# The last down projection as seven block products, with the weights' block sums made in DRAM

## The chip, the cores and the metric

The kernel runs on one core of one Trainium2 chip. The metric is the device time of the program in microseconds. Three runs of the kernel before gave a median of 1703.05 us (1701.98 to 1703.95).

## The reference, cut to what matters

The program is two layers of a transformer block on 512 tokens of width 1024, in float32. Each layer has a mixer of four branches (causal attention with forget decay, dilated attention, retention and latent attention, MLA), gates, an output projection, and a feed-forward block:

```
h = rms_norm(x, g_pre_ffn[l])
f = (silu(h @ w_ffn_gate[l]) * (h @ w_ffn_up[l])) @ w_ffn_down[l]     # [512,2816] @ [2816,1024]
x = x + rms_norm(f, g_post_ffn[l])
```

The change concerns the last line of the product, `... @ w_ffn_down[l]`, in the second (last) layer. It is the last matrix product of the program; the norm, the residual sum and the store of the output follow it.

## The kernel before, in words

**Products.** A float32 operand is split in two float32r parts: `hi` is a copy by ACT (ScalarE) and `lo = x - hi` is a subtraction by DVE (VectorE) or, for some tiles, by POOL (GpSimd). A product of two such pairs takes three matmuls (hi hi, hi lo, lo hi), which `mm3` and its relatives issue.

**Weights.** All weights lie in one DRAM array `wts` in the order in which they are used. `w_load` loads them by DMAs on SP's queue into three buffers `raw`, `conversion` splits each into `whi` and `wlo`, and `take` hands out the next tile with two more converted ahead. So SP's queue carries the weights, and among them other transfers, above all `move` (L1060), which copies halves of query and key tiles within SBUF.

**Order of the work.** `collect` runs the main chain of products (projections, gates, output projection, feed-forward block) and, at a spacing, steps of a background list `self.bg` (attention and retention), first in, first out. A scheduler (Tile) then orders each engine's instructions: it places an instruction where, by its own estimate of times, the engine is free and the instruction's inputs are there; it holds to the written order in the stretches that `ordered` marks, on the engines named there. Every engine and every queue then runs its instructions in the order in which they stand.

**POOL's part.** In the first 100 us POOL splits the `lo` of query and key tiles (`split_to`, L484, called by `queries` and `keys`), then of value tiles (`v_split`, L930), then multiplies the attention weights by their reciprocal sums (`normalise`, L653). PE transposes the result (L660). SP's moves of the query and key halves (L1062) wait for the splits. In the feed-forward block POOL also issues accumulating DMAs (`units_load`, L335), which add one weight tile to another while loading.

**The feed-forward block.** The gate and up products already run in seven block products in place of eight (`quarter_products`), for 18 of the 22 tiles of the hidden width; the sums of weights for it come partly by these accumulating DMAs into SBUF, partly from DVE. The hidden tiles are held as float32.

**The last product.** `split_rest` (L1671) splits the 22 hidden tiles, and `finish` (L1693) computes the output in token layout: four column blocks of 256, each for four token blocks over 22 tiles of the hidden width, three matmuls each, so 4 x 4 x 22 x 3 = 1056 matmuls of 256 columns. Squares for the norm are summed after each block; the last block's evacuation (`evac`, c == 3) takes the root, scales, adds the residual `xt` and stores.

Of the kernel before, what the change touches and what calls it, by code (L numbers as in the profile page):

```python
# [16 lines left out]
LAYERS = 2  # L17
# [33 lines left out]
NR = 8  # L51
HQ = 3
AHEAD = 2
LAST_K = ((0, 2), (2, 2), (4, 2), (6, 2), (8, 4), (12, 4), (16, 4), (20, 2))

# [10 lines left out]
def plan():  # L66
# [6 lines left out]
    for l in range(LAYERS):  # L73
# [36 lines left out]
        if l < LAYERS - 1:  # L110
            for d, k0, nk in DOWN:
                add("down", nk, 128, lambda a, l=l, d=d, k0=k0, nk=nk:
                    _ktiles(a["w_ffn_down"][l], k0, nk, np.arange(d * 128, d * 128 + 128)))
        else:
            for c in range(4):
                for k0, nk in ((0, 4), (4, 4), (8, 4), (12, 4), (16, 4), (20, 2)) if c < 3 else LAST_K:
                    add("held" if c == 3 and nk == 2 and k0 < 8 else "downt", nk, 256, lambda a, l=l, c=c, k0=k0, nk=nk:
                        _ktiles(a["w_ffn_down"][l], k0, nk, np.arange(c * 256, c * 256 + 256)))
    return out
# [86 lines left out]
class Builder:  # L206
# [28 lines left out]
    def stream_init(self):  # L235
        self.wi = 0
        self.n_dma = self.n_conv = 0
        self.woff = [0]
        for _, nk, nc, _ in self.plan:
            self.woff.append(self.woff[-1] + 128 * nk * nc)  # L240
        self.raw, self.whl = {}, {}
        self.n_held = 0

# [27 lines left out]
    def conversion(self, lo_engine=None):  # L271
# [6 lines left out]
        kh = (nk + 1) // 2  # L278
        if name == "held":
            kh = nk  # L280
            if self.n_held < 2:
                t2 = self.hp.tile([128, 1024], F32R, tag="fraw", name="held")
                tiles = [(t2[:, 0:512], t2[:, 512:1024])]
            else:
                tiles = [(self.ar(), self.ar())]
            self.n_held += 1
        else:
            hi = self.whi.tile([128, 1024], F32R, tag="whi", name="whi")
            lo = self.wlo.tile([128, 1024], F32R, tag="wlo", name="wlo")
            tiles = [(hi, lo), (hi[:, kh * ncol:], lo[:, kh * ncol:])][:nk]  # L290
        ws = [], []
# [28 lines left out]
    def units_load(self, upto):  # L320

        nc = self.nc
        groups = (FT - CM) // 2
        while self.n_unit <= min(upto, 5 * groups - 1):
            g, n = divmod(self.n_unit, 5)
            if self.n_unit % NR < RB:
                t = self.wraw.tile([128, 1024], F32, tag="raw", name="raw")
            else:
                t = self.hp.tile([128, 1024], F32, tag="fraw", name="raw")
            a11, a21, a12, a22 = (self.ap["wts"][self.woff[i]:self.woff[i + 1]].rearrange("(p n) -> p n", p=128)  # L330
                                  for i in range(self.n_dma + 4 * g, self.n_dma + 4 * g + 4))
# [5 lines left out]
            self.n_unit += 1  # L337
        if upto >= 5 * groups:
# [3 lines left out]
            self.w_load(self.n_dma + upto - 5 * groups)  # L342

    def quarters_ahead(self, n):
# [4 lines left out]
        if not self.q_todo:  # L349
# [3 lines left out]
    def quarters_init(self):  # L353

        groups = (FT - CM) // 2
        self.q_todo, self.q_done, self.q_used = deque(), 0, 0
# [5 lines left out]
        for g in range(groups):  # L362
            self.q_todo.extend(self.quarter_steps(5 * g))

    def quarter_steps(self, u):
        nc = self.nc
        st = {}

        def plain(src):
            hi = self.whi.tile([128, 1024], F32R, tag="whi", name="whi")  # L370
            lo = self.wlo.tile([128, 1024], F32R, tag="wlo", name="wlo")
            nc.scalar.copy(hi, src)  # L372
            nc.vector.tensor_sub(lo, src, hi.bitcast(F32))  # L373
            self.quarter.append((hi, lo))

# [810 lines left out]
    def project(self, l, u):  # L1186
# [52 lines left out]
        for i in range(2):  # L1239
# [344 lines left out]
    def ffn(self, l, u, ps, y, xt=None):  # L1584
# [8 lines left out]
        ops = None  # L1593
        self.quarters_init()
        for m in range(CM):
# [96 lines left out]

    def finish(self, hid, xt):  # L1693

        nc = self.nc
        y = {}
        ss, before = self.small(16), self.small(4)
        gout = [self.a(), self.a()]
        for h in range(2):
            nc.sync.dma_start(gout[h], self.ap["gout"][:, 512 * h:512 * h + 512])  # L1700

        for c in range(4):
            def evac(t, ps, c=c):
                half, o = c // 2, 256 * (c % 2)
                if c % 2 == 0:
                    y[t, half] = self.a()
                j = self.a()
                nc.scalar.activation(j[:, 0:256], ps, AF.Square, accum_out=ss[:, 4 * t + c:4 * t + c + 1])
                nc.vector.tensor_mul(y[t, half][:, o:o + 256], ps, gout[half][:, o:o + 256])
                if c == 2:  # L1710
                    s1 = before[:, t:t + 1]
                    nc.vector.tensor_reduce(s1, ss[:, 4 * t:4 * t + 3], axis=mybir.AxisListType.X, op=ALU.add)
                    nc.vector.scalar_tensor_tensor(s1, s1, 1.0 / D, self.eps[:, t:t + 1], op0=ALU.mult, op1=ALU.add)
                if c == 3:
                    s1, r, t1 = (self.small(1) for _ in range(3))
                    nc.vector.scalar_tensor_tensor(s1, ss[:, 4 * t + 3:4 * t + 4], 1.0 / D, before[:, t:t + 1],
                                                   op0=ALU.mult, op1=ALU.add)
                    for _ in self.root(s1, r, t1):
                        pass
                    for h in range(2):  # L1720
                        f = y[t, h]
                        nc.vector.scalar_tensor_tensor(f, f, r, xt[t, h], op0=ALU.mult, op1=ALU.add)
                        nc.sync.dma_start(self.out[128 * t:128 * t + 128, 512 * h:512 * h + 512], f)

            if c < 3:
                tags = ("b",) * 4 if c % 2 == 0 else ("acc", "acc", "acc", "b")
                for r in self.tm("downt", hid, 256, (4, 4, 4, 4, 4, 2), tags):
                    if r == 3:
                        yield 3
                    else:  # L1730
                        evac(*r)
                continue
            ws = {}
            for k0, nk in LAST_K:
                w = self.take("held" if nk == 2 and k0 < 8 else "downt")
                for k in range(nk):
                    ws[k0 + k] = w[0][k], w[1][k]
            for t in range(4):
                o = self.ps("b")[:, 0:256]
                ts = slice(128 * t, 128 * t + 128)  # L1740
                mm = nc.tensor.matmul
                for k in range(FT):
                    x, w = hid[k], ws[k]
                    mm(o, x[0][:, ts], w[0], start=k == 0, stop=False)
                    mm(o, x[0][:, ts], w[1], start=False, stop=False)
                    mm(o, x[1][:, ts], w[0], start=False, stop=k == FT - 1)
                evac(t, o)
                yield 3

    def build(self):  # L1750
        nc, tc = self.nc, self.tc
        with ExitStack() as ctx:
# [26 lines left out]
            for l in range(LAYERS):  # L1779
# [12 lines left out]
                with tc.tile_pool(name="fraw%d" % l, bufs=NR - RB) as self.hp, tc.tile_pool(name="hid%d" % l, bufs=HQ) as self.hq:  # L1792
                    xt = None
                    if last:
                        xt = {}
                        self.bg.append(("xt", self.to_tokens(x, xt)))
                    hid = self.collect(self.ffn(l, u, ps, x, xt))
                    del u, x
                    hid = self.split_rest(hid)
                    x = self.bring_back()  # L1800
                    if last:
                        self.run(self.finish(hid, {(k // 2, k % 2): x[k] for k in range(KT)}))
                    else:
                        u, x = self.down_block(hid, lambda d: self.vec("post_ffn", 8 * l + d), x,
                                         lambda k: self.vec("pre_mix", 8 * (l + 1) + k))
# [62 lines left out]
```

## Time and profile before

| | |
|---|---|
| median of three runs | 1703.05 us |
| profiled execution, time | 1705.07 us |
| profiled execution, span | 1703.3 us |
| granted TensorE clock, mean | 0.998 of full |
| PE busy / weight loads | 1674.1 us (98%) / 1503.2 us (88%) |
| DVE / ACT / POOL busy | 1086.8 (64%) / 823.0 (48%) / 335.6 us (20%) |
| DMA | 217.47 MB, mean 128 GB/s |

The span is the time from the first to the last instruction of the profiled execution; its time, 1705.07 us, has 1.77 us around it, and is 2.02 us above the median of the runs. Busy shares are means over the span: PE is busy almost everywhere. The other engines, the DMA queues and the waits matter where PE waits for them.

### The profile page before, as it was taken

Reading aid. Unit: us, or ns where it says so; the run is one execution under the profiler, and the core shown is the slowest. Engines: PE = TensorE matmul, PEld = TensorE weight load, DVE = VectorE, ACT = ScalarE, POOL = GpSimd, SP = SyncE. Lnnn points to the kernel's source line nnn. Section 1 sums busy time; section 2 is a strip of 40 time slices with the busy share of each in tenths; the row PEclk is TensorE's granted clock in tenths of the full one; section 3 lists DMA queues with packets and bytes.
Section 4 is the critical chain, followed back from the end, with each engine's and each line's share of the span. In section 5 each row is a group of like instructions: output and inputs, shape, how many; then the busy total and the mean of one; then the engine's idle time right before and its main releaser. Section 6 shows DMA issues by size and latency. Waiting matters only on the chain.

```text
span 1703.3 us, 27371 instructions
## 1 busy us (share of the span) xinstructions
PE 1674.1 (98%) x10340; PEld 1503.2 (88%) x10340; DVE 1086.8 (64%) x2078; ACT 823.0 (48%) x1657; POOL 335.6 (20%) x344
## 2 busy tenths in 40 slices
PE   9999999999999999999998999999999999999998
PEld 7788888888898999988887988788888989999998
DVE  6657777555468777752485578664554787777423
ACT  6566653323455555553355656432334555555422
POOL 0144333222130010000212443422222300000000
PEclk9999999999999999999999999999999999999999
DMA  5633325323434666243245442343234267773421
GB/s 185 191 106 118 100 81 158 96 93 100 157 114 129 185 180 185 87 160 101 65 153 159 116 115 81 100 155 99 93 99 155 63 185 187 182 178 84 165 94 57
DMA packets 75780, 217.47 MB, mean 128 GB/s; under 512 B 9728, under 2 KB 9984, under 8 KB 75648
## 3 DMA queue, kind: packets, MB, share of 16 engines
q1 hardware_dynamic: 70464, 196.85, 36.3%
q0 software_dynamic: 5184, 18.88, 6.5%
q8 instruction: 81, 1.33, 0.3%
q14 instruction: 51, 0.42, 0.1%
HBM read 189.47 MB, written 8.39 MB: 116 GB/s over the span
## 4 chain that ended last, share of the span: by engine, by line
PE 61%; DVE 4%; ACT 1%; issue 1%; DMA 1%; POOL 0%; DVEq 0%; ACTq 0%
PE acc L491 8%; PE acc L492 8%; PE acc L493 8%; PE acc L465 4%; PE acc L467 4%; PE acc L466 4%; PE b L467 3%; PE b L466 3%; PE b L465 3%; PE b L980 1%; PE b L982 1%; PE b L981 1%; PE b L714 1%; DVE wlo L298 1%; PE b L634 1%
## 5 line engine op out<-in xcount | busy, mean ns | idle before, releaser
L491 PE MATMUL acc<-a,whi 128*128 128x512 f32 (+1 forms) x1238 | 478.0, 386 | 0.0
L493 PE MATMUL acc<-a,wlo 128*128 128x512 f32 (+1 forms) x1238 | 469.4, 379 | 0.0
L492 PE MATMUL acc<-a,whi 128*128 128x512 f32 (+1 forms) x1211 | 459.1, 379 | 0.0
L297 ACT CAST whi<-raw 128x512 fp32r<-128x512 f32 (+3 forms) x442 | 237.5, 577 | 392.4 <-issue 162.1
L298 DVE TENSOR_TENSOR wlo<-raw,whi 128x512 fp32r<-128x512 f32 (+3 forms) x442 | 301.2, 713 | 183.2 <-ACT whi L297 182.1
L493 PEld LDWEIGHTS acc<-a,wlo 128*128 128x128 f32 x1238 | 233.3, 188 | 44.1 <-issue 0.5
L491 PEld LDWEIGHTS acc<-a,whi 128*128 128x128 f32 x1238 | 234.0, 189 | 38.7 <-issue 1.0
L492 PEld LDWEIGHTS acc<-a,whi 128*128 128x128 f32 x1211 | 228.6, 189 | 38.8 <-DVE a L487 0.6
L465 PE MATMUL acc<-a,whi 128*128 128x256 f32 x560 | 158.5, 283 | 1.9 <-DVE a L1598 1.5
L466 PE MATMUL acc<-a,whi 128*128 128x256 f32 x560 | 158.4, 283 | 0.0
L467 PE MATMUL acc<-a,wlo 128*128 128x256 f32 x560 | 158.2, 283 | 0.0
L373 DVE TENSOR_TENSOR wlo<-raw,whi 128x1024 fp32r<-128x1024 f32 x90 | 110.2, 1225 | 57.1 <-ACT whi L372 53.5
L372 ACT CAST whi<-raw 128x1024 fp32r<-128x1024 f32 x90 | 94.4, 1049 | 95.1 <-PE acc L466 47.0
L1261 DVE TENSOR_TENSOR a<-acc,a 128x512 f32<-128x512 f32 x64 | 44.2, 691 | 137.2 <-PE acc L493 137.2
L465 PE MATMUL b<-a,whi 128*128 128x256 f32 x448 | 126.8, 283 | 0.0
L466 PE MATMUL b<-a,whi 128*128 128x256 f32 x448 | 126.8, 283 | 0.0
L467 PE MATMUL b<-a,wlo 128*128 128x256 f32 x448 | 126.8, 283 | 0.0
L1280 POOL TENSOR_TENSOR a<-a 128x512 f32<-128x512 f32 x48 | 70.3, 1467 | 237.8 <-DVE a L1279 229.1
L465 PEld LDWEIGHTS acc<-a,whi 128*128 128x128 f32 x560 | 107.4, 192 | 2.3 <-ACT whi L372 1.7
L466 PEld LDWEIGHTS acc<-a,whi 128*128 128x128 f32 x560 | 107.5, 192 | 0.1
L467 PEld LDWEIGHTS acc<-a,wlo 128*128 128x128 f32 x560 | 107.4, 192 | 0.0
L335 POOL DMA_DIRECT2D raw<-wts x36 | 31.2, 868 | 354.8 <-DMA raw<-wts 195.6
(293 smaller groups left out, 3398.0 us busy)
## 6 DMA issues: line engine op xcount, KB each, us to landing
raw<-wts SPq DMA_DIRECT2D x260, 512.0 KB, 3.6
raw<-wts POOLq DMA_DIRECT2D x36, 512.0 KB, 6.2
a<-a SPq DMA_DIRECT2D x120, 128.0 KB, 2.3
raw<-wts SPq DMA_DIRECT2D x40, 256.0 KB, 2.6
a<-xT SPq DMA_DIRECT2D x16, 256.0 KB, 6.4
away<-a SPq DMA_DIRECT2D x16, 256.0 KB, 6.8
a<-away SPq DMA_DIRECT2D x16, 256.0 KB, 4.9
raw<-wts SPq DMA_DIRECT2D x7, 452.0 KB, 3.8
```

The source lines that it names most:

```text
L297: todo.append(lambda hi=hi, src=src, n=n: nc.scalar.copy(hi[:, :n], src))
L298: todo.append(lambda hi=hi, lo=lo, src=src, n=n: (lo_engine or nc.vector).tensor_sub(lo[:, :n], src, hi[:, :n].bitcast(F32)))
L372: nc.scalar.copy(hi, src)
L373: nc.vector.tensor_sub(lo, src, hi.bitcast(F32))
L465: mm(o, hi[:, c], x[k][0], start=first, stop=False, skip_group_check=i in (2, 3, 4, 6))
L466: mm(o, hi[:, c], x[k][1], start=False, stop=False, skip_group_check=i in (2, 3, 4, 6))
L467: mm(o, lo[:, c], x[k][0], start=False, stop=k == 3, skip_group_check=i in (2, 3, 4, 6))
L491: mm(out, w[0], x[0], start=start, stop=False)
L492: mm(out, w[0], x[1], start=False, stop=False)
L493: mm(out, w[1], x[0], start=False, stop=stop)
L1261: nc.vector.tensor_mul(z, ps, self.rB)
L1280: nc.gpsimd.tensor_add(merged[dd], merged[dd], t)
```

## The change

The last product is done by blocks. The 512 tokens are cut into two halves, the 2816 rows of hidden width into two times 11 tiles (`FH`), and the 1024 columns into two times 512. Seven products of one half block each (11 tiles, 2 token blocks of 128, 512 columns, three matmuls: 66 matmuls; 462 in all, of 512 columns) take the place of eight. Four of the seven use sums of weight blocks, called p, q, r and v: p = a21+a22, r = a11+a21, q = p+a11, v = q+a12. `make_sums` makes them in a new DRAM array `sums`: for each sum six DMAs on POOL's queue copy the first term, and six accumulating DMAs add the second (48 DMAs; in each six, five of 512 KB and one of 256 KB, so 5.5 times 512 KB), every one cut into pieces of 256 float32 (`max_dma_last_dim=1024`, 512 rows of 1 KB). They are put on the background list behind the last layer's retention and drained before its feed-forward block. `w_load` no longer serves the last product; `units_load` loads its blocks, the sums among them, as plain tiles from DRAM. The sums of hidden tiles (t1 to t4) are made by DVE in `finish`, whose operands are split product by product, so `split_rest` is not called for the last layer. The residual `xt` comes back from DRAM in the fourth product.

```diff
+OPS = 3
+LATE = 8
+FH = FT // 2
+LAST_K = tuple((k, min(2, FH - k)) for k in range(0, FH, 2))
...
-            for c in range(4):
-                for k0, nk in ((0, 4), (4, 4), (8, 4), (12, 4), (16, 4), (20, 2)) if c < 3 else LAST_K:
...
+            for c, k1 in ((0, 0), (0, FH), (512, 0), (512, FH)):
+                for k0, nk in LAST_K:
+                    add("block", nk, 512, lambda a, l=l, c=c, k=k0 + k1, nk=nk:
+                        _ktiles(a["w_ffn_down"][l], k, nk, np.arange(c, c + 512)))
...
+    def make_sums(self):
+
+        a11, a12, a21, a22 = (self.block_quarter(n) for n in range(4))
+        p, q, r, v = (self.block_sum(n) for n in "pqrv")
+        for dst, first, more in ((p, a21, a22), (r, a11, a21), (q, p, a11), (v, q, a12)):
+            for d, f in zip(dst, first):
+                self.nc.gpsimd.dma_start(d, f, max_dma_last_dim=1024)
+                yield
+            for d, m in zip(dst, more):
+                self.nc.gpsimd.dma_start(d, m, accum_op=ALU.add, max_dma_last_dim=1024)
+                yield
+
+    def block_sources(self):
+        a11, a12, _, a22 = (self.block_quarter(n) for n in range(4))
+        return [*a11, *a12, *self.block_sum("q"), *self.block_sum("r"), *a22, *self.block_sum("p"), *self.block_sum("v")]
...
         self.bg.append(("b%d" % RET, self.retention(self.heads(q, k), v, g, self.br[RET], l)))
+        if l == LAYERS - 1:
+            self.bg.append(("sums", self.make_sums()))
...
+        products = (plain(0, h0), plain(FH, h0), of_t2, of_t3, of_t4, of_t1, plain(FH, h1))
...
+        for n in range(7):
+            first, grouped = n in (0, 1, 5), n in (2, 3, 4, 6)
...
+            for k, nk in steps:
+                operands(OPS)
+                self.quarters_ahead(AHEAD)
+                w = self.quarter.popleft()
...
+                held.append((k, nk, ready.popleft(), w))
+                if k >= LATE:
+                    continue
+                self.block(banks[n], held.pop(), (0, 1), first, grouped)
+            for t in range(2):
+                for x in held:
+                    self.block(banks[n], x, (t,), first, grouped)
+                after(n)(t)
...
+            self.sums = dram.tile([4, 128 * 512 * FH], F32, name="sums")
...
                     if last:
+                        self.drain("sums")
                         xt = {}
```

**POOL, the start of the program.** This is what stood first in POOL's queue before; `a` are the work tiles, `sm1` the reciprocal sums, L484 the splits of queries and keys, L930 those of values, L653 the scaling of attention weights.

```order
L484 TENSOR_TENSOR a_443<-a_440,a_442 128x512 [waits Activation_49]
L484 TENSOR_TENSOR a_517<-a_514,a_516 128x512 [waits Activation_49]
L484 TENSOR_TENSOR a_610<-a_607,a_609 128x512 [waits Activation_49]
L484 TENSOR_TENSOR a_695<-a_692,a_694 128x512 [waits Activation_49,Pool_49]
L930 TENSOR_TENSOR a_811<-a_809,a_811 128x4x64 [waits PE_49,Activation_49]
L930 TENSOR_TENSOR a_816<-a_814,a_816 128x4x64 [waits PE_49,Activation_49]
L930 TENSOR_TENSOR a_889<-a_887,a_889 128x4x64 [waits DMAHW5_49,Activation_49]
L930 TENSOR_TENSOR a_894<-a_892,a_894 128x4x64 [waits Activation_49]
L653 TENSOR_SCALAR a_919<-a_919,sm1_939 128x128 [waits DVE_49,PE_49]
L653 TENSOR_SCALAR a_934<-a_934,sm1_957 128x256 [waits DVE_49]
```

The first split of a query tile was POOL's first work of any length.

Now 34 DMAs of the sums stand ahead of that split (L522 is the old L484). This fence begins with the 31st of the 48; L360 copies, L363 accumulates, and the semaphores DMASW are those of POOL's own DMAs.

```order
L363 DMA sums_86<-wts 512x256 [waits DMASW6_49,DMASW0_49]
L363 DMA sums_86<-wts 512x256 [waits DMASW7_49,DMASW1_49]
L363 DMA sums_86<-wts 512x256 [waits DMASW2_49]
L363 DMA sums_86<-wts 512x256 [waits DMASW3_49]
L522 ISA
L522 TENSOR_TENSOR a_444<-a_441,a_443 128x512 [waits Activation_49]
L363 DMA sums_86<-wts 512x256 [waits DMASW4_49]
L522 TENSOR_TENSOR a_518<-a_515,a_517 128x512 [waits Activation_49]
L363 DMA sums_86<-wts 256x256 [waits DMASW5_49]
```

The scheduler has put the DMAs, which need nothing but weights in DRAM, at the head of POOL's queue in the first layer, though the program writes them in the second. The last of them stand here, with what follows (L968 is the old L930, L691 the old L653):

```order
L522 TENSOR_TENSOR a_611<-a_608,a_610 128x512 [waits Activation_49]
L363 DMA sums_86<-wts 512x256 [waits DMASW5_49]
L363 DMA sums_86<-wts 512x256 [waits DMASW6_49]
L363 DMA sums_86<-wts 512x256 [waits DMASW7_49]
L363 DMA sums_86<-wts 512x256 [waits DMASW0_49]
L363 DMA sums_86<-wts 256x256 [waits DMASW1_49]
L522 TENSOR_TENSOR a_696<-a_693,a_695 128x512 [waits DMAHW0_49,Activation_49]
L968 TENSOR_TENSOR a_812<-a_810,a_812 128x4x64 [waits PE_49,Activation_49]
L968 TENSOR_TENSOR a_817<-a_815,a_817 128x4x64 [waits PE_49,Activation_49]
L968 TENSOR_TENSOR a_890<-a_888,a_890 128x4x64 [waits DMAHW5_49,Activation_49]
L968 TENSOR_TENSOR a_895<-a_893,a_895 128x4x64 [waits PE_49,Activation_49]
L691 TENSOR_SCALAR a_920<-a_920,sm1_940 128x128 [waits DVE_49]
```

All 48 stand ahead of the fourth split and of the first scaling of attention weights; each waits for the DMA eight places ahead of it (or a later one) and, where it accumulates or reads a sum, for the one that wrote it.

**SP, the same place of the program.** Before, the moves of query halves (L1062) stood among the weight loads (L257) thus:

```order
L836 DMA a_467<-ukv 128x512 [waits DMAHW3_49]
L257 DMA raw_533<-wts 128x1024 [waits DMAHW4_49,DVE_49]
L257 DMA raw_621<-wts 128x1024 [waits DMAHW5_49,DVE_49]
L257 DMA raw_706<-wts 128x1024 [waits DVE_49]
L1062 DMA a_520<-a_516 64x512 [waits DMAHW7_49,Activation_49]
L1062 DMA a_520<-a_517 64x512 [waits DMAHW0_49,Pool_49]
L257 DMA raw_714<-wts 128x1024 [waits DMAHW4_49,DMAHW1_49,DVE_49]
L1062 DMA a_516<-a_517 64x512 [waits DMAHW7_49,DMAHW2_49]
L257 DMA raw_897<-wts 128x1024 [waits DMAHW5_49,DMAHW3_49,DVE_49]
```

Now (L1100 is the old L1062, L259 the old L257):

```order
L259 DMA raw_622<-wts 128x1024 [waits DMAHW4_49,DVE_49]
L259 DMA raw_707<-wts 128x1024 [waits DMAHW5_49,DVE_49]
L259 DMA raw_715<-wts 128x1024 [waits DMAHW6_49,DVE_49]
L1100 DMA a_447<-a_444 64x512 [waits Pool_49]
L1100 DMA a_443<-a_444 64x512 [waits DMAHW7_49]
L1100 DMA a_521<-a_517 64x512 [waits DMAHW0_49,Activation_49]
L1100 DMA a_521<-a_518 64x512 [waits DMAHW1_49,Pool_49]
L259 DMA raw_898<-wts 128x1024 [waits DMAHW3_49,DMAHW2_49,DVE_49]
L1100 DMA a_517<-a_518 64x512 [waits DMAHW0_49]
```

The three weight loads stand a little earlier, ahead of the first move that waits for POOL; the loads behind it wait with it.

## Rows read from the trace of the kernel before

**Rows 1.** Who waited for whom: total us, times, longest; PE, whole span.

```profile
PE b L660 <- POOL a L653: 4.7, 6, 1.8
```

**Rows 2.** Timeline of PE near 88 us: start, duration, [idle before it <- releaser].

```profile
87.18 0.44 PE L634 MATMUL b<-a 128*128 128x128 f32 x3
88.75 0.33 PE L660 MATMUL b<-ct,a 128*128 128x128 f32 x1 [1.13 <-POOL a L653]
```

**Rows 3.** Timeline of POOL, first 90 us.

```profile
42.94 2.09 POOL L484 TENSOR_TENSOR a<-a 128x512 fp32r<-128x512 f32 x1 [42.49 <-ACT a L483]
...
74.35 1.29 POOL L484 TENSOR_TENSOR a<-a 128x512 fp32r<-128x512 f32 x1 [5.88 <-ACT a L483]
81.41 1.82 POOL L930 TENSOR_TENSOR a<-a 128x256 fp32r<-128x256 f32 x2 [5.76 <-ACT a L929]
85.36 1.60 POOL L930 TENSOR_TENSOR a<-a 128x256 fp32r<-128x256 f32 x2 [2.14 <-ACT a L929]
88.33 0.37 POOL L653 TENSOR_SCALAR a<-a,sm 128x128 f32<-128x128 f32 x1 [1.37 <-DVE sm L652]
```

**Rows 4.** Timeline of SP's queue, first 100 us.

```profile
59.95 0.33 SPq L257 DMA_DIRECT2D raw<-wts  x1
...
79.39 2.89 SPq L257 DMA_DIRECT2D raw<-wts  x2
```

**Rows 5.** Busy us of each engine, clock, DMA share and GB/s by stretch.

```profile
core 0: us, PE busy (x) PEld busy (x) DVE busy (x) ACT busy (x) POOL busy (x), PEclk, DMA share, GB/s
...
0.00:88.80 88.80, 80.72 (x413) 68.32 (x414) 56.86 (x129) 52.44 (x107) 9.84 (x13) 1.00 0.57 180
```

**Rows 6.** DMA queues of the page: packets, MB, share of 16 engines' span.

```profile
q1 hardware_dynamic: 70464, 196.85, 36.3%
q0 software_dynamic: 5184, 18.88, 6.5%
```

**Rows 7.** Line L335, POOL's accumulating DMAs: ns min/median/max, and us to landing.

```profile
L335 POOL DMA_DIRECT2D raw<-wts x36: 853/862/1021, 283.0 to 1531.9; - x36
...
DMA to landing us min/median/max: 5.2/6.2/9.6
```

**Rows 8.** DMA in 40 slices of 856 to 866 us: busy tenths, GB/s (stores to DRAM).

```profile
DMA  9899878999999999999999999899432110200000
GB/s 410 328 328 344 311 279 344 320 385 410 377 393 385 410 410 402 434 410 393 402 385 377 393 410 369 311 401 410 148 139 98 74 74 0 66 0 0 0 0 0
...
kept<-a SPq DMA_DIRECT2D x8, 256.0 KB, 4.0
```

**Rows 9.** Timeline of PE: a stretch of 512 columns, first and last of 14.

```profile
61.42 0.39 PE L491 MATMUL b<-a 128*128 128x512 f32 x1
...
64.42 0.39 PE L492 MATMUL b<-a 128*128 128x512 f32 x1
```

**Rows 10.** Timeline of PE: first and last matmul of the last product.

```profile
1569.29 0.28 PE L980 MATMUL b<-whi,a 128*128 128x256 f32 x1
...
1696.17 0.28 PE L1746 MATMUL b<-whi,h 128*128 128x256 f32 x1
```

**Rows 11.** Groups of DVE, 1440 us to the end: busy us, mean ns.

```profile
L373 DVE TENSOR_TENSOR wlo<-raw,whi 128x1024 fp32r<-128x1024 f32 x30 | 36.8, 1225 | 19.8 <-ACT whi L372 18.9 <-ACT a L1623 0.4
...
L484 DVE TENSOR_TENSOR a<-a 128x512 fp32r<-128x512 f32 x16 | 10.1, 687 | 0.1
...
L1722 DVE SCALAR_TENSOR_TENSOR a<-a,sm 128x512 f32<-128x512 f32 x8 | 5.7, 749 | 0.1
L1709 DVE TENSOR_TENSOR a<-b,a 128x256 f32<-128x256 f32 x13 | 5.4, 422 | 19.8 <-ACT a L1708 19.6
```

**Rows 12.** Timeline, the last work of DVE.

```profile
1698.72 1.41 DVE L1722 SCALAR_TENSOR_TENSOR a<-a,sm 128x512 f32<-128x512 f32 x2
```

**Rows 13.** Timeline of PE at the program's start.

```profile
5.87 0.74 PE L1002 MATMUL acc<-whi,a 128*128 128x452 f32 x1 [0.50 <-ACT a L1307]
...
10.97 0.58 PE L1003 MATMUL acc<-wlo,a 128*128 128x452 f32 x1
...
11.35 0.58 PE L1004 MATMUL acc<-whi,a 128*128 128x452 f32 x1
...
12.20 0.37 PE L1004 MATMUL acc<-whi,a 128*128 128x452 f32 x1
...
12.40 0.37 PE L1002 MATMUL acc<-whi,a 128*128 128x452 f32 x1
```

More of the change, by code (lines that the diff above doesn't have):

```diff
@@ L278, in conversion @@
         kh = (nk + 1) // 2
[L279 to L290, printed above, removed]
+        hi = self.whi.tile([128, 1024], F32R, tag="whi", name="whi")
+        lo = self.wlo.tile([128, 1024], F32R, tag="wlo", name="wlo")
+        tiles = [(hi, lo), (hi[:, kh * ncol:], lo[:, kh * ncol:])][:nk]
         ws = [], []
@@ L337, in units_load @@
             self.n_unit += 1
-        if upto >= 5 * groups:
+        if upto >= 5 * groups and not self.blocks:
             if self.n_unit == 5 * groups:
@@ L1593, in ffn @@
         ops = None
-        self.quarters_init()
+        self.quarters_init(self.block_sources() if xt is not None else [])
         for m in range(CM):
@@ L1691, in to_tokens, with finish @@
                 yield
-    def finish(self, hid, xt):
+    def finish(self, h):
         nc = self.nc
-        y = {}
-        ss, before = self.small(16), self.small(4)
[L1698 to L1748, printed above, removed]
@@ new lines, in finish, with operands @@
+        products = (plain(0, h0), plain(FH, h0), of_t2, of_t3, of_t4, of_t1, plain(FH, h1))
+        beside = {0: make_t1, 1: make_t2}
+        todo = deque((f, k, nk) for f in products for k, nk in LAST_K)
+        ready = deque()
+        def operands(n):
+            while todo and len(ready) < n:
+                f, k, nk = todo.popleft()
+                ready.append(f(k, nk))
+        chain, other, late = ([self.ps(t), self.ps(t)] for t in ("b", "b", "acc"))
+        banks = (chain, other, chain, chain, chain, late, late)
@@ new lines, in finish, with done @@
+        e = {n: [self.a(), self.a()] for n in (0,)}
+        y, xt = {}, {}
+        ss, before = self.small(16), self.small(4)
+        def done(t, half, src, sign, at):
+            j = self.a()
+            c = 4 * t + half
+            nc.scalar.activation(j, src, AF.Square, accum_out=ss[:, c:c + 1])
+            y[t, half] = self.a()
+            stt(y[t, half], src, sign, gout[half], op0=ALU.mult, op1=ALU.mult)
+            if not at:
+                nc.vector.scalar_tensor_tensor(before[:, t:t + 1], ss[:, c:c + 1], 1.0 / D, self.eps[:, t:t + 1],
+                                               op0=ALU.mult, op1=ALU.add)
+                return
+            s1, r, t1 = (self.small(1) for _ in range(3))
+            nc.vector.scalar_tensor_tensor(s1, ss[:, c:c + 1], 1.0 / D, before[:, t:t + 1], op0=ALU.mult, op1=ALU.add)
+            for _ in self.root(s1, r, t1):
+                pass
+            for i in range(2):
+                f = y.pop((t, i))
+                stt(f, f, r, xt.pop((t, i)), op0=ALU.mult, op1=ALU.add)
+                nc.sync.dma_start(self.out[128 * t:128 * t + 128, 512 * i:512 * i + 512], f)
@@ new lines, in block @@
+    def block(self, banks, step, ts, first, grouped):
+        mm = self.nc.tensor.matmul
+        k0, nk, x, w = step
+        for t in ts:
+            for i in range(nk):
+                c = slice(256 * i + 128 * t, 256 * i + 128 * t + 128)
+                ws = slice(512 * i, 512 * i + 512)
+                last = k0 + i == FH - 1
+                mm(banks[t], x[0][:, c], w[0][:, ws], start=first and k0 + i == 0, stop=False, skip_group_check=grouped)
+                mm(banks[t], x[0][:, c], w[1][:, ws], start=False, stop=False, skip_group_check=grouped)
+                mm(banks[t], x[1][:, c], w[0][:, ws], start=False, stop=last, skip_group_check=grouped)
```

130 lines of the change are left out of this document (113 added, 17 removed).

## The prediction

> **What bounds the kernel now.** I read the page first: PE is busy nearly everywhere, so a saving must come off PE's work, and whatever makes PE wait is added to the time in full. Next I read who waits for whom on PE. Its waits are short, and the one on another engine that the change touches is PE's wait for POOL: the transposes of the attention weights (L660) wait for POOL's scaling (L653), 4.7 us in six waits [rows 1]. So I looked at where that chain begins. PE's first such transpose is at 88.75 us, right behind POOL's first scaling [rows 2]; POOL did little before, and mostly waited for ACT, 42.49 us ahead of its first split [rows 3]. To a scheduler that is a free engine. Then I set the new order of POOL's queue beside these times: 34 of the 48 DMAs of the sums now stand ahead of the split that ran at 42.94 us, and all 48 ahead of the one that ran at 74.35 us. The question of the whole change is when the chip can be done with them. The last stretch I read last: PE goes through the old product without a gap [rows 10].
>
> **The end: what the seven products save.** The old product has 1056 matmuls of 256 columns. The first starts at 1569.29 and the last at 1696.17, 1055 steps of 0.1203 us, so 127.0 us in all [rows 10]. Matmuls of 512 columns follow each other by (64.42 - 61.42) / 13 = 0.2308 us [rows 9]; 462 of them take 106.6 us. PE saves 20.4 us.
>
> DVE gets more to do beside it. Weights: 35 splits of 1024 columns at 1.225 us and 7 of 512 at 0.69, 47.7 us. Operands: three products split plainly, 33 halves at 0.42, and four from sums, 4 x (5 x 0.687 + 0.42), 29.3 us. Sums of hidden tiles: 44 halves at 0.42, 18.5 us. Evacuations: 4 sums at 0.69 and 8 products with the gain at 0.75, 8.8 us [rows 11]. That is 104 us of DVE beside 106.6 us of PE, and the norm and final scaling of the first two token blocks (some 5 us) come on top. DVE is then as full as PE, with a few tiles of lead (three operand sets, two weight tiles), and ACT must come first for each split. I count 6 us of PE's waits for it (0 if the lead covers all, 15 if DVE runs a seventh slower than its sum). The 22 splits ahead of the old product, 22 x 0.687 = 15.1 us, fall away, but PE had not waited for them, so they are worth nothing.
>
> The tail grows. Before, the last matmul ended at 1696.17 + 0.28 and DVE's last instruction at 1698.72 + 1.41, 3.7 us later [rows 10, 12]. Now two token blocks are finished close together, 2 x (0.69 + 0.75 + about 1.1 of small steps + 1.41) = 7.9 us of DVE, of which the first may start nine matmuls (2.1 us) before the end: about 6 us, 2.3 more than before. So the end gives 20.4 - 6 - 2.3 = 12.1 us, between 3 and 18.
>
> **The start: what the sums cost.** POOL runs its queue in order. The fourth split stands behind the last accumulate, and this waits for the sixth copy of v, the 42nd DMA. Up to that one there are four rounds of copies and three of accumulates, each round 5.5 times 512 KB: 22 copies and 16.5 accumulates of 512 KB. No row shows a copy from DRAM to DRAM, nor 1 KB pieces. Bounds for 512 KB with all 16 engines:
>
> Copies. Stores to DRAM in 2 KB pieces move up to 410 GB/s [rows 8], which makes 1.28 us the low end. The high end is the mean packet of the hardware queue, 0.363 x 1703.3 x 16 / 70464 = 0.140 us [rows 6], taken for every 1 KB piece: 512 pieces and 16 completions are 33 packets on each engine, 4.63 us.
>
> Accumulates. The 36 of the old kernel took 0.065 x 1703.3 / 36 = 3.08 us of all engines each, in 144 packets of 0.342 us [rows 6, 7]. Low end 3.08 us (bytes decide), high end 33 x 0.342 = 11.3 us (packets decide).
>
> The 2 KB row shows no loss against the bigger pieces, so I stay nearer the bytes than the packets, but not at them, as each piece is half as long again and both ends are DRAM: 0.067 us a piece for a copy, 2.2 us, and 0.150 for an accumulate, 5.0 us. The sum is 22 x 2.2 + 16.5 x 5.0 = 130.9 us of the DMA engines (78.9 at the low ends, 287.9 at the high ends).
>
> The other traffic goes on beside it until PE stops: the share was 0.57 over the first 88.8 us [rows 5], 50.6 us. The 42nd DMA has then landed at 130.9 + 50.6 = 181.5 us. Behind it on POOL come one issue (0.86 [rows 7]), the fourth split (1.29), the four value splits (3.42) and the first scaling (0.37) [rows 3]: 187.4 us. PE wanted that scaling at 88.75, so it stands still for 98.7 us. What else waits there costs nothing more: SP's weight load that went at 59.95 is now behind a move that waits for POOL's second split, and the next (79.39) behind the fourth [rows 4], but the tiles already loaded reach past PE's stop. A slower first 20 us, with the sums in the loads' way, is hidden too, since POOL is later still. Nor is the wait won back later, because PE has no slack to give.
>
> After such a pause PE may begin at its lower clock. At the start of the program steps of 0.38 us went over to 0.20, as from 1.2 to 2.4 GHz, after about 5.9 us of work [rows 13]; that lost 5.9 x (1 - 0.205 / 0.375) = 2.6 us, and I add it once.
>
> The Trainium skill, page "DMA: Bandwidth & Descriptors", section "Latency and other measured facts", gives 207 to 214 GB/s for well-pitched copies between HBM tensors. By it 512 KB would take 2.45 us; with accumulates dearer by the ratio of the two queues' bytes, 1.87, the estimate for the sums would be 129 us, so nearly the same time; no run so far shows such a copy.
>
> **Sum.** 1705.07 + 98.7 + 2.6 - 12.1 = 1794.3 us for a profiled execution like this one. That execution lay 2.0 us above the median of the runs, so I predict 1792 us.
>
> **Rivals.** *A, the forecast:* the wait at middle prices, 1765 to 1860 us. For it: the order of POOL's queue and the row of PE waiting for POOL.
>
> *B, bytes decide.* At the low ends the 42nd DMA lands at 129.5 us, PE waits 46.7 us, and the time is 1703.05 + 46.7 - 18 = 1732 us. For it speaks the 2 KB row; against it that every piece is 1 KB, and that POOL must write four times as many descriptors: if an issue grows from 0.862 us with the packets (528 against 144, 3.16 us), 44 full issues alone take 139 us and the time is 1750 us.
>
> *C, packets decide.* At the high ends PE waits 255.6 us and the time is 1703.05 + 255.6 + 2.6 - 3 = 1958 us. For it: an accumulate that reads and writes DRAM has a round trip in each piece; against: the 2 KB row.
>
> *D, the other side, faster.* The change does what its background place intends: the sums are over before POOL is needed. That takes all 42 DMAs within 88.75 - 5.9 = 82.8 us, of which the rest uses 50.6, so 32 us for what costs 78.9 at the lowest rows. The end's gain is eaten once the sums take over 44 us. If it came so, the time would be 1703.05 - 12.1 = 1691 us. Only if the busy share of the engines overstates what they were doing could it be.
>
> **How the numbers follow.** A 0.55, B 0.22, C 0.16, D 0.05, and 0.02 for a wait that just cancels the gain. The bounds of the unknown prices run from 1732 to 1958. The range 1735 to 1900 leaves out D, the low tip of B and the upper half of C, together under 0.2. One measurement of this kernel can tell 0.2% (3.4 us) from no change: faster 0.05, same 0.02, slower 0.93.
>
> **What would show it.** Right: PE's first transpose of attention weights has an idle time of 50 us or more in front, released by POOL; POOL's first split comes after 34 DMAs, well past 42.94; the stretch behind is shifted as a whole; the last product takes about 107 to 115 us with steps of 0.23 us; DVE is above 90% busy there. Wrong: POOL's first scaling runs near 88 us (D), or the time between issue and landing of the sums' DMAs is far off 2.2 and 5.0 us per 512 KB in the mean, once the queue is full (B or C), or PE stops for the end's operands rather than for POOL at the start.

## The result, and the profile after

The changed kernel takes 1728.05 us (median of 4 runs) against 1703.14 us beside it: a ratio of 1.0147, 95% interval 1.0134 to 1.016. It is slower, as forecast, but by 25 us and not by 89; the time lies 7 us below the range. The profiled execution took 1727.95 us, with a span of 1726.2.

**The start.** The timeline of POOL answers to [rows 3], in its columns: the first split, the fourth, the first scaling, and ahead of them the last two accumulates (`x2`), of which the second, about 1 us later, waits for the 42nd DMA.

```profile
88.80 1.67 POOL L522 TENSOR_TENSOR a<-a 128x512 fp32r<-128x512 f32 x1
...
118.38 1.93 POOL L363 DMA_DIRECT2D sums<-wts  x2 [0.35 <-DMA sums<-sums]
119.97 1.63 POOL L522 TENSOR_TENSOR a<-a 128x512 fp32r<-128x512 f32 x1
121.19 3.10 POOL L968 TENSOR_TENSOR a<-a 128x256 fp32r<-128x256 f32 x4
123.94 1.15 POOL L691 TENSOR_SCALAR a<-a,sm 128x128 f32<-128x128 f32 x2
```

The first scaling is 35.6 us later than before (88.33). PE's first transpose of attention weights [rows 2] follows it at 124.69:

```profile
124.69 0.47 PE L698 MATMUL b<-ct,a 128*128 128x128 f32 x1 [4.65 <-POOL a L691]
```

PE did not stop for 36 us in one piece, though; the idle time released by POOL is 4.65. It had been slow from the first microseconds. The stretches (the columns of [rows 5]) show it: 33 matmuls in the first 20 us where there were 57, and 308 up to 88.8 us where there were 413, at a granted clock of 0.90.

```profile
0.00:20.00 20.00, 12.41 (x33) 8.09 (x34) 6.06 (x10) 6.05 (x9) 11.34 (x18) 0.96 0.93 305
0.00:88.80 88.80, 69.95 (x308) 57.08 (x309) 44.84 (x106) 40.53 (x80) 27.33 (x39) 0.90 1.08 295
88.80:124.00 35.20, 22.09 (x116) 18.02 (x115) 12.60 (x26) 13.74 (x30) 19.51 (x24) 0.76 1.13 266
```

How much of the delay was there before POOL decided anything is seen at four casts of ACT whose inputs come from PE, not from POOL. Of ACT's line (ns min/median/max, first and last start), before:

```profile
L483 ACT CAST a<-b x4: 581/581/582, 61.6 to 71.1; 64x512 fp32r<-64x512 f32 x4
```

and after:

```profile
L521 ACT CAST a<-b x4: 581/581/582, 80.3 to 90.4; 64x512 fp32r<-64x512 f32 x4
```

They are 19 us late, and POOL's first split began only at 88.80. So some 19 us were lost ahead of POOL, and from there it is POOL that comes last: between 60 and 126 us ACT waits for its split, and PE for the rows that follow from it (total us, times, longest).

```profile
PE b L672 <- DVE a L968: 9.2, 2, 5.8
...
ACT a L967 <- POOL a L522: 6.9, 1, 6.9
```

The DMAs of the first 118.4 us say why, in the queues' columns of [rows 6] and with the median us to landing of three kinds of issue:

```profile
q0 software_dynamic: 12382, 20.64, 76.0%
q1 hardware_dynamic: 5473, 13.62, 32.6%
...
sums<-wts POOLq DMA_DIRECT2D x30, 512.0 KB, 17.1
raw<-wts SPq DMA_DIRECT2D x11, 512.0 KB, 9.9
...
a<-xT SPq DMA_DIRECT2D x8, 256.0 KB, 13.7
```

In the same stretch of the kernel before, x (`a<-xT`) landed after 5.6 us and weights after 4.6:

```profile
raw<-wts SPq DMA_DIRECT2D x16, 512.0 KB, 4.6
...
a<-xT SPq DMA_DIRECT2D x8, 256.0 KB, 5.6
```

Of the whole page, the software queue's row answers to [rows 6]:

```profile
q0 software_dynamic: 20032, 41.95, 12.9%
```

**The end.** First and last matmul of the new product [rows 10], and DVE's last work [rows 12]:

```profile
1604.83 0.40 PE L1890 MATMUL b<-whi,a 128*128 128x512 f32 x1
...
1717.01 0.39 PE L1892 MATMUL acc<-whi,a 128*128 128x512 f32 x1
```

```profile
1721.61 1.41 DVE L1828 SCALAR_TENSOR_TENSOR a<-a,sm 128x512 f32<-128x512 f32 x2
```

The product begins 35.54 us later than before, so of what was lost in the first 124 us nothing was won back, and nothing added to it, in the 1480 us between. From there to the end of the span it takes 1726.2 - 1604.8 = 121.4 us, against 1703.3 - 1569.3 = 134.0: a gain of 12.6.

### The profile page after: what moved, and what is told of

It is laid out like the page before. It is cut to its first block, busy times and chain, and to the rows that moved or that the text cites. A ratio compares the mean times of both kernels' runs of the same rounds, so it can differ in the third digit from the quotient of the medians.

```text
span 1726.2 us, 26398 instructions
## 1 busy us (share of the span) xinstructions
PE 1665.4 (96%) x9746; PEld 1469.8 (85%) x9746; DVE 1130.4 (65%) x2145; ACT 849.7 (49%) x1676; POOL 373.4 (22%) x392
## 4 chain that ended last, share of the span: by engine, by line
PE 59%; DVE 4%; ACT 1%; issue 1%; POOL 1%; DMA 1%; SPq 0%; DVEq 0%; ACTq 0%
PE acc L529 8%; PE acc L530 8%; PE acc L531 8%; PE acc L503 4%; PE acc L505 4%; PE acc L504 4%; PE b L505 3%; PE b L504 3%; PE b L503 3%; PE b L1890 2%; PE b L1892 1%; PE b L1891 1%; PE b L752 1%; DVE wlo L291 1%; PE b L672 1%
## 5 line engine op out<-in xcount | busy, mean ns | idle before, releaser
L290 ACT CAST whi<-raw 128x512 fp32r<-128x512 f32 (+3 forms) x398 | 213.6, 577 | 353.0 <-PE acc L530 154.8
L291 DVE TENSOR_TENSOR wlo<-raw,whi 128x512 fp32r<-128x512 f32 (+3 forms) x398 | 273.9, 719 | 151.2 <-ACT whi L290 150.7
L531 PEld LDWEIGHTS acc<-a,wlo 128*128 128x128 f32 x1238 | 233.9, 189 | 43.9 <-issue 0.5
L529 PEld LDWEIGHTS acc<-a,whi 128*128 128x128 f32 x1238 | 234.4, 189 | 38.6 <-issue 1.0
L405 DVE TENSOR_TENSOR wlo<-raw,whi 128x1024 fp32r<-128x1024 f32 x132 | 157.6, 1195 | 67.8 <-ACT whi L404 63.7
L404 ACT CAST whi<-raw 128x1024 fp32r<-128x1024 f32 x132 | 135.4, 1027 | 127.1 <-PE acc L504 51.2
L521 ACT CAST a<-a 128x512 fp32r<-128x512 f32 (+1 forms) x143 | 77.6, 567 | 75.2 <-DVE a L860 20.4
```

What stands on the lines that cost most here:

```text
L290: todo.append(lambda hi=hi, src=src, n=n: nc.scalar.copy(hi[:, :n], src))
L291: todo.append(lambda hi=hi, lo=lo, src=src, n=n: (lo_engine or nc.vector).tensor_sub(lo[:, :n], src, hi[:, :n].bitcast(F32)))
L404: self.nc.scalar.copy(hi, src)
L405: self.nc.vector.tensor_sub(lo, src, hi.bitcast(F32))
L529: mm(out, w[0], x[0], start=start, stop=False)
L531: mm(out, w[1], x[0], start=False, stop=stop)
```

## Experiments

The theory: the loss is all at the start and the gain all at the end, and POOL's order (its splits and scalings behind the sums' DMAs) makes the loss. The rival: the sums' bytes hold back the loads, whatever POOL's order.

**End only, and start only.** The first takes `make_sums` out and gives the last product plain blocks in place of q, r, p and v:

```diff
-            self.bg.append(("sums", self.make_sums()))
-        return [*a11, *a12, *self.block_sum("q"), *self.block_sum("r"), *a22, *self.block_sum("p"), *self.block_sum("v")]
+        return [*a11, *a12, *a21, *a11, *a22, *a21, *a12]
```

> The changed kernel without the 48 DMAs that make the sums: the last product takes plain blocks (a11, a12, a21, a22) where it took q, r, p and v, so its numbers are not the reference's, but each instruction of the end stands as in the changed kernel. Theory (the loss is all at the start, the end gains what its two traces say, 134.0 - 121.4 = 12.6 us): 1703.1 - 12.6 = 1690.5 us, between 1688 and 1693; the last product begins at about 1569 us and POOL's first split is back at about 43 us. Rival (the end gains nothing, or less, when the work ahead of it is not late): 1700 to 1704 us.

The second adds `make_sums` and its place in `project` to the kernel before, and changes nothing else.

> The kernel before with the 48 DMAs of the sums added at the same place of the program; nothing reads the sums, and the last product is the eight-block one. Theory (POOL runs them ahead of its first split, and everything behind it is late by 35.5 us): 1703.1 + 35.5 = 1738.6 us, between 1734 and 1743; first split at about 89 us, first scaling of POOL at about 124 us (88.33 before). Rival (the DMAs cost nothing by themselves, the loss is in the new last product and its loads): 1703 to 1708 us.

End only: 1688.64 us against 1701.65, ratio 0.9922 (0.9907 to 0.9936). Start only: 1738.04 us, ratio 1.0216 (1.0199 to 1.0233). Their product is 1.0136, inside the interval of the change (1.0134 to 1.016). So there are two parts, -13.0 and +36.4 us, and no third that these runs can tell (the interval is some 4 us wide).

**Held back.** Each sums' DMA is queued behind one of POOL's 48 additions in the gate stages:

```diff
-                        nc.gpsimd.tensor_add(merged[dd], merged[dd], t)
+                        add = nc.gpsimd.tensor_add(merged[dd], merged[dd], t)
+                        with self.tc.issue_after(add.ins):
+                            next(self.todo, None)      # todo = make_sums()
```

> The changed kernel with the 48 DMAs held back: one is queued on POOL behind each of its 48 additions in the two layers' gate stages (about 13.6 us for two of them), in place of all 48 ahead of POOL's first split. All else is the changed kernel's. Theory (it is their place in POOL's order that costs): POOL's first split back at about 43 us, PE no later, 1703.1 - 12.6 = 1690.5 us, up to 1695 if the weights of the gates come a little later beside them; faster than both kernels. Rival (the bytes cost the time wherever they are moved, through the DMA engines that the weights need): 24 x 2.0 + 24 x 3.1 = some 110 us of packets in stages whose share is 0.37 to 0.56 would again show as weights that come late, 1710 to 1728 us. In this run the queue's share while only copies or only accumulates run gives the price of each alone: 2.0 us and 3.1 us for 512 KB if the split made from the changed kernel's totals is right, 2.2 and 5.0 if the forecast's prices were right.

1691.88 us, ratio 0.9937 (0.9922 to 0.9952): faster than both. POOL's first scaling is back at 88.06 us. Here each kind of DMA runs by itself, with the DMA engines about half busy, so each has a price. Software queue, 379.5 to 419.5 us (five copies of 512 KB and one of 256 KB, so five and a half):

```profile
q0 software_dynamic: 800, 2.88, 20.8%
```

and 420 to 520 us (five accumulates and a half):

```profile
q0 software_dynamic: 2912, 2.88, 19.8%
```

A copy of 512 KB takes 0.208 x 40 / 5.5 = 1.51 us of all engines, an accumulate 0.198 x 100 / 5.5 = 3.60: neither the 2.0 and 3.1 expected here nor the forecast's 2.2 and 5.0. The accumulates went in 1 KB packets (5 x 528 + 272 = 2912), the copies did not: 800 packets are 5 x 144 + 80, so 144 a copy, as with 4 KB pieces, though the code asks for 1 KB.

**Early, but spread.** The same with one DMA behind each of POOL's first 48 splits and scalings in the first layer, so that nothing stands ahead of the first split.

> The changed kernel with the 48 DMAs between POOL's instructions of the first layer's attention: one behind each of its first 48 splits and scalings (from about 43 us on), none ahead of the first split. Theory (the wait for POOL behind its DMAs costs, the traffic beside the first loads costs little): POOL never holds more than one DMA ahead of a split, at most some us per DMA where it has eight in flight and has to wait for one; 1691 to 1700 us, the first splits and scalings at about their times of before (43, 74, 88 us). Rival (the traffic itself delays the first layer's loads, whatever POOL's order): 1705 to 1728 us with POOL's splits waiting for ACT and PE, and x and weight loads that land 10 us or more after their issue.

1726.14 us, ratio 1.0139 (1.0124 to 1.0154): my theory's number was wrong, the rival's right. POOL's first scaling ran at 89.01 us, but between 100 and 200 us, where most of the DMAs now were, PE did 419 matmuls in place of 613 (this run, then the kernel before):

```profile
100.00:200.00 100.00, 79.63 (x419) 68.34 (x419) 46.84 (x129) 42.91 (x107) 58.16 (x71) 0.88 1.10 269
```

```profile
100.00:200.00 100.00, 99.07 (x613) 88.36 (x612) 66.65 (x172) 59.73 (x150) 42.69 (x51) 1.00 0.41 116
```

The software queue took 85.3% of that stretch, 128 KB moves (a<-a) landed after 6.2 us in place of 2.3. So POOL's order was not the only cause, and the next runs took order, issue and bytes apart.

**An eighth of the bytes, at the start and early.** 16 of each DMA's 128 rows; first on "start only", then on "early" (there with the plain blocks of "end only"):

```diff
-                self.nc.gpsimd.dma_start(d, f, max_dma_last_dim=1024)
+                self.nc.gpsimd.dma_start(d[:16], f[:16], max_dma_last_dim=1024)
```

> The kernel before with the 48 DMAs at the start, as in the run of the start alone (1738.0 us), but each moves an eighth of its bytes (16 of 128 rows, 64 KB in place of 512 KB); nothing reads the sums. POOL's own time to issue them stays: 24 x 0.6 + 24 x 1.0 = some 39 us, from 1.3 us on, with few waits for landings. Theory (POOL is late since the 42nd DMA lands late, by the packets of 512 KB each): the first split at 43 to 48 us, 1701.7 + 0 to 5 = 1702 to 1707 us. Rival (what POOL needs to issue 48 DMAs costs the time, with their bytes hidden): 1715 to 1738 us.

> The kernel with one DMA behind each of POOL's first 48 splits and scalings (1726.1 us), with an eighth of the bytes in each DMA, and the last product from plain blocks (the sums are not read). POOL's issues stay, 39 us of it spread over 43 to 195 us, each between two instructions that PE waits for in turn. Theory now, since 1691 to 1700 was wrong there (the bytes beside the first layer's loads and copies cost by themselves; landings of 128 KB copies a<-a rose from 2.3 to 6.2 us): 1689 to 1694 us. Rival (POOL's issue time between the scalings is on PE's path: PE waited 11.7 us for them): most of the 34 us remains, 1710 to 1726 us. Half and half would be 1695 to 1710.

At the start 1702.82 us, ratio 0.9999 (0.999 to 1.0008): issuing the 48 DMAs, 34 of them ahead of the first split, costs nothing by itself. The first split and the first scaling stand where they stood (42.94 and 88.33):

```profile
42.97 2.10 POOL L507 TENSOR_TENSOR a<-a 128x512 fp32r<-128x512 f32 x1 [12.21 <-ACT a L506]
...
88.30 0.37 POOL L676 TENSOR_SCALAR a<-a,sm 128x128 f32<-128x128 f32 x1 [1.29 <-DVE sm L675]
```

Early 1693.23 us, ratio 0.9953 (0.9938 to 0.9968) against 0.9922 for "end only": some 5 us at most (give or take 4) for the issues between scalings. The other 32 of the 37 us between "early" and "end only" go with the bytes.

**Bytes without POOL's order.** Eight large copies (2.75 MB each, read by nobody) are added to the kernel before; eight can be in flight, so POOL waits for none. Once at the start, once behind POOL's first eight instructions.

```diff
+            for i in range(8):
+                end = self.woff[-1] - i * n                # n = 128 * 512 * FT // 2
+                nc.gpsimd.dma_start(sums[i].rearrange("(p n) -> p n", n=1024),
+                                    self.ap["wts"][end - n:end].rearrange("(p n) -> p n", n=1024), max_dma_last_dim=4096)
```

> The kernel before with traffic alone: POOL issues eight large copies at the start (2.75 MB each, DRAM to DRAM in pieces of 4 KB, read by nobody) and then has nothing to wait for, since eight DMAs fit in flight. 44 times 512 KB at 1.65 us = some 73 us of packet time, against some 112 us of the 48 sums' DMAs. POOL's first split can run at 43 us. Theory A (POOL's order alone): 1702 to 1707 us. Theory B (traffic by itself): 73/112 x 35.5 = 23 us late, 1718 to 1730 us, the first copies and weights landing 10 us or more after their issue (x 5.6 us and weights 4.6 us without it).

> The kernel before with the eight large copies (2.75 MB each, 73 us of packet time, read by nobody) at the place of the early DMAs: one behind each of POOL's first eight instructions, from 43 to 88 us, in place of all at the start (1731.6 us, 28 late). No instruction of POOL waits for a landing, since only eight are in flight. Theory (the traffic beside the first layer's attention is what cost the version with the early DMAs its 34 us): 73/112 x 34 = 22 us late, 1717 to 1733 us. Rival (POOL's waits for landings between its scalings cost it, traffic as such nothing there, since x and the first weights have landed): 1703 to 1710 us.

At the start: 1731.6 us, ratio 1.0164 (1.0149 to 1.0179), 28 us late with POOL free, just above the expected range. It waits for ACT, and ACT for what the loads bring late:

```profile
1.27 5.50 POOL L1770 DMA_DIRECT2D sums<-wts  x8 [0.82 <-POOLq L1865]
63.91 1.29 POOL L484 TENSOR_TENSOR a<-a 128x512 fp32r<-128x512 f32 x1 [57.14 <-ACT a L483]
...
116.75 0.37 POOL L653 TENSOR_SCALAR a<-a,sm 128x128 f32<-128x128 f32 x1 [1.37 <-DVE sm L652]
```

Its x landed after 15.6 us. From 43 us on: 1718.24 us, ratio 1.0091 (1.0076 to 1.0106), 16 late. The copies took less packet time than the 73 us expected: 60.0% of 40 to 140 us, so 60 us, against 60.3% of 40 to 220 us, so 109, for the sums' DMAs in "early". If the loss goes by packet time, which is an estimate, that makes 16 x 109 / 60 = 29 of the 37 us. With 5 for the issues 3 are left, less than the intervals tell; POOL also waited 11.9 us for landings ahead of its DMAs there, and what these waits cost no run took apart.

**POOL's order without bytes.** POOL scales a tile that nothing reads, ahead of its first split (N1 times) and between the third and fourth (N2 times); no DMA is added.

```diff
+N1, N2 = 190, 58          # second run: 152, 16
+            self.held = self.nc.gpsimd.tensor_scalar(self.idle, self.idle, 1.0, 1.0, op0=ALU.mult, op1=ALU.mult)
```

> The kernel before, with POOL kept busy on a tile that nothing reads, with no DMA added: 190 scalings of 128x256 ahead of its first split and 58 more between its third and fourth, so that the first split starts near 89 us and the fourth near 120, as they did behind the sums' DMAs (88.80 and 119.97). Theory A (POOL's order alone makes the loss of 35.5 us: PE waits for what POOL does late): some 1702 + 35 = 1737 us, at least 1728. Theory B (the sums' traffic holds back the loads and the copies that PE, ACT and DVE need, POOL's lateness is beside it): less than half of it, 1702 to 1718 us. If the two overlap (each alone makes most of the loss, together no more): this run 1725 to 1737 and the run with traffic alone late too.

> The kernel with POOL kept busy and no DMA added (1776.8 us) again, with fewer idle scalings, since each took 0.567 us where 0.45 was taken: 152 ahead of the first split (1.2 + 152 x 0.567 = 87.4 us) and 16 (9 us) ahead of the fourth, so that POOL's first scaling comes near the 123.94 us of the changed kernel (88.33 before; 166.87 with 190 and 58). Theory (PE is late by what POOL's first scalings are late): 1703 + 32 to 38 = 1735 to 1741 us, if the second and third split wait for ACT no longer than before; 1725 to 1735 if they don't. Rival (the stall costs only where the traffic delays the loads too): 1705 to 1720 us.

The first held too long (0.567 us a scaling): 1776.82 us, ratio 1.0432, first real scaling at 166.87. The second, ratio 1.0238 (1.0221 to 1.0255), 1742.66 us, 40 late and just above the expected range, with the first real scaling at 133.06 and not near 123.94:

```profile
89.01 1.26 POOL L493 TENSOR_TENSOR a<-a 128x512 fp32r<-128x512 f32 x1
...
123.00 1.74 POOL L493 TENSOR_TENSOR a<-a 128x512 fp32r<-128x512 f32 x1
...
133.06 0.37 POOL L666 TENSOR_SCALAR a<-a,sm 128x128 f32<-128x128 f32 x1 [1.67 <-PE acc L506]
```

Here PE runs as before up to 60 us and then stops in one piece, as the forecast had it (stretch 60 to 88 us; who waited for whom on PE):

```profile
60.00:88.00 28.00, 0.13 (x2) 0.00 (x0) 0.00 (x0) 0.00 (x0) 23.30 (x58) 0.58 0.00 0
```

```profile
PE b L881 <- DVE a L1070: 38.8, 1, 38.8
```

The time lost is 0.90 of what the scaling is late (40.3 of 44.7 us), in the first run 0.93 (73.3 of 78.5): without traffic too, PE pays for POOL's order nearly in full. But the stop goes through SP's queue. A move (a<-a) waits there for the first split, and the loads behind it wait too:

```profile
51.87 38.88 SPq L1075 DMA_DIRECT2D a<-a  x2
90.80 1.08 SPq L848 DMA_DIRECT2D a<-uq  x2
```

In the changed kernel these loads stand elsewhere in SP's queue and went at 55.31 us. So the two runs show that a late POOL is enough by itself, but not what it would cost by itself in the changed kernel's own order of SP's queue. Traffic alone cost 28 us (with 62 us of packet time), order alone 40, both together 36.4: they overlap.

**Accumulates in 4 KB pieces**, at the start and held back:

```diff
-                self.nc.gpsimd.dma_start(d, m, accum_op=ALU.add, max_dma_last_dim=1024)
+                self.nc.gpsimd.dma_start(d, m, accum_op=ALU.add, max_dma_last_dim=4096)
```

> The changed kernel with the accumulates in pieces of 4 KB in place of 1 KB (128 pieces for 512 KB, as the copies' packets are, in place of 512); all else as it was. Theory (packet time sets when the 42nd DMA lands): an accumulate of 512 KB takes 3.1 us as the old ones into SBUF (110.7 us for 36) in place of 3.6 (19.8 us for 5.5 in the run with late DMAs), so 16.5 x 0.5 = 8 us less packet time ahead of the first scaling, which at a queue share of 0.76 is some 11 us of the clock: 1728 - 11 = 1717 us, between 1713 and 1722. Rival (bytes alone, or the number of DMAs, decide): 1726 to 1730 us. POOL's issue of one stays at 1.0 us if it doesn't go by pieces.

> The version with the DMAs behind the gate stages' additions (1691.9 us), with accumulates in pieces of 4 KB. Theory: they are off every path there, so 22 x 0.5 = 11 us less of packet time change nothing that can be measured: 1689 to 1693 us, landing of an accumulate 5.5 us in place of 6.3. Rival (the traffic beside the gates' weights still costs the 3 us by which that version was behind the one without the DMAs, 1688.6): 1687.5 to 1689.5 us.

At the start 1724.8 us, ratio 1.0131 (1.0117 to 1.0144): 3 us, not 11, and the interval overlaps that of the change. The packet time fell as expected (70.0% of 118.4 us in place of 76.0%: 7.1 us), and POOL's last accumulate went at 112.97 in place of 118.38. But now POOL was not what came last:

```profile
L521 ACT CAST a<-b x4: 581/581/582, 94.8 to 104.8; 64x512 fp32r<-64x512 f32 x4
```

```profile
122.32 1.55 POOL L968 TENSOR_TENSOR a<-a 128x256 fp32r<-128x256 f32 x2 [2.99 <-ACT a L967]
125.16 0.37 POOL L691 TENSOR_SCALAR a<-a,sm 128x128 f32<-128x128 f32 x1 [1.29 <-DVE sm L690]
```

The casts are 33 us late where they were 19 late in the changed kernel, weights landed after 14.2 us in place of 9.9, and POOL waits for ACT. What POOL's order gave back, the loads took.

Held back, 1689.65 us, ratio 0.9925 (0.9912 to 0.9939), within its interval the time of "end only", and the fastest version that makes and uses the sums. An accumulate took 3.05 us (16.8% of 420 to 520 us). That it beats the 1 KB version (0.9922 to 0.9952) is not shown.

## Why the prediction was right or wrong

**The end was right.** Forecast 12.1 us, measured 12.6 in the traces and 13.0 by leaving the sums out. (In the traces of "end only" and of both held-back versions the product and its tail took 119.7 or 119.8 us in place of 121.4; that difference was not taken apart.) PE's waits inside the product were 4.8 us (2.7, 1.2 and 0.9, for ACT and DVE) where 6 were counted; the last matmul ends at 1717.40 and DVE at 1723.02, a tail of 5.6 us for 6. One sign failed: DVE was to be above 90% busy there, and was busy for 95.3 of 112.6 us (85%).

**The order at the start was right, the time of it not.** POOL did run the DMAs first, and the 42nd released the last accumulate; from the last two accumulates to the first scaling it took 123.94 - 118.38 = 5.6 us, where 5.9 were counted. The step that failed is "The 42nd DMA has then landed at 130.9 + 50.6 = 181.5 us": it had landed within about 1 us of 118.4. The 63.1 us between 118.4 and 181.5 fall into three:

- The prices. 5.0 us for an accumulate was 3.6, and 2.2 for a copy was 1.51: 16.5 x 1.4 + 22 x 0.69 = 38 us too much. The queue itself shows 0.760 x 118.4 = 90.0 us for 130.9, so 40.9 (some of its packets are already those of the last accumulates). The two errors have one root each: an accumulate's 1 KB packet took 3.6 x 16 / 528 = 0.109 us and not 0.150, and the copy was not cut to 1 KB at all.
- The other traffic. 50.6 us was its share in a program that runs at full speed. PE was slowed, asked for less, and it was 0.326 x 118.4 = 38.6: 12.0.
- The addition. The shares come to 1.086 of the time, so packets of the two queues overlap here, and their times must not be added as if one waited for the other: 10.2.

With 118.4 for 181.5 in the forecast's own sum the time is 1705.07 + 118.4 + 5.9 - 88.75 - 12.1 - 2.0 = 1726.5 us (the clock's 2.6 lies inside the stretch). That it comes so near 1728 does not show POOL to be the only cause, as the next paragraph says. Rival B's 1732 us came near by luck: it had too little for the sums (78.9 us for 90.0), too much for the other traffic, added whole (50.6), and too much for the end (18 for 12.6). Its issue-bound variant (3.16 us for 528 packets) fell: an issue took 1.02 us, a copy's 0.62.

**The path to PE's loss was half wrong too.** The forecast had PE standing still for POOL in one wait, of 50 us or more, and "A slower first 20 us, with the sums in the loads' way, is hidden too". PE's wait for POOL was 4.65 us; some 19 of its 36 us were lost ahead of POOL, on loads that came late, and the traffic alone cost 28 us with POOL free. In the time this did not show, since the two delays lie in the same stretch and end close together. I named one cause where there were two, each enough for most of the loss (POOL's order as far as the runs with idle scalings show it); the version that undid only the one (early) showed it.

The Trainium skill, page "DMA: Bandwidth & Descriptors", section "SWDGE vs HWDGE vs iDMA", says that software and hardware queues feed different queues inside each DMA engine and that the engine takes turns between them. The landings here agree: with the sums in flight SP's weights took 9.9 us in place of 4.6, though no sum stood in SP's queue. The 207 to 214 GB/s that the forecast quotes from the Trainium skill (the same page, section "Latency and other measured facts") were measured for tiles of 128 rows of 16 KiB on the sync and scalar queues; the 2.45 us for 512 KB that it works out from 214 is not the price of these contiguous copies on POOL's queue, for which 1.51 us were measured, 347 GB/s.

## What to carry to other kernels

DMAs without inputs can be scheduled to the front of their engine's queue, as all 48 were here, and then they move their bytes in just the stretch where the program waits for its first loads; tie them to an instruction in a stage where the DMA engines have room (here 1728 us became 1690). When a delay has a queue and a transfer that end close together, undo each by itself before naming the cause. Price a DMA from its packets in a trace, not from the piece size in the code. A sum that meets the measured time does not show that its path was the only one.

## What the runs showed of the hardware that was not expected

- POOL's time to issue a DMA hardly follows its size: 0.62 us for a copy of 512 KB, 0.69 for one of 2.75 MB in 704 pieces; accumulates 1.02 us in 1 KB pieces, 0.81 in 4 KB.
- A copy from DRAM to DRAM took 1.4 us of all 16 engines for 512 KB in the copies of 2.75 MB at the start (61.8 / 44) and 1.51 in the held-back sums, half an accumulate of the same size in 4 KB pieces (3.05).
- With both queues full the shares of the 16 engines came to 1.02 (copies alone in the software queue) to 1.13 (with accumulates in 1 KB packets).
- In the second run with idle scalings PE stood idle from 60.1 to 98.9 us, and its granted clock from 60 to 97 us was 0.56 in the mean. Behind the pause it still ran at the lower of its two levels (1.2 GHz): steps of 256 columns took 0.21 us up to 102.2 and 0.12 behind it, and twelve of them 2.66 us in place of 1.44. So this pause of 38.8 us cost some 1.2 us more than its length.
